# A two-layer hybrid mixer on one core: four PSUM banks for background projections, a reordered inverse, and paired low-rank products

## The chip, the core and the metric

The kernel runs on one core of one Trainium2 chip. The metric is the device time of one execution in microseconds (us); lower is better. PE is the matmul engine (PEld is its weight load), DVE the vector engine, ACT the scalar engine, POOL the GpSimd engine, SP the engine that issues most DMA transfers. PSUM, into which PE writes, has 8 banks of 128 partitions by 512 float32.

## What is computed

Two layers of a diffusion backbone over 768 tokens (256 context, then 512 latent) of width 1024. In each layer four mixers read one normalised input through one large projection `w_in`; each mixer's result is lifted to width 1024, weighted by a sigmoid gate that is also computed from the input, summed, and projected again; an MLP follows. The mixer that matters here is branch B, a bidirectional recurrence with four heads of 64:

```python
# per direction d, per head; kk is the normalised key, b = kk * a
w = -softplus(-(w0[d] + tanh(wl) @ w2[d])) - 0.5          # decay
a = sigmoid(a0[d] + al @ a2[d])                           # rate
S_t = S_{t-1} (diag(exp(-exp(w_t))) - kk_t^T b_t) + v_t^T k_t
y_t = S_t r_t
```

`wl` and `al` hold 64 columns for the forward and 64 for the backward direction, and so do the rows of `w2` and `a2`.

## The kernel before, in words

**Products in three parts.** Nearly all projections take a split of both operands into a high and a low float32r part and three matmuls per 128 rows (`mm3_steps`, all recorded at line 387). Weights come by DMA from SP in halves of 128x512 (tile `wr`), ACT casts the high part (`wh`, line 258) and POOL or DVE subtracts for the low part (`wl`, line 259). Four raw and four split halves are kept, which is two projections' worth.

**Background work.** Branch B has long serial stretches. To fill PE, `fill(t)` draws steps from generators: `spill` (projections of other mixers, rotated, split and stored to DRAM), `gates`, `ada_steps` (the modulation vectors, 16 loads and 8 row additions each, mixed into `spill`), and `decays`. A projection's result sits in a PSUM tile `pm` of the pool `psm` (2 banks) until ACT copies it out (`st`, line 504, or `gate`). The call `fill` stands at fixed places of branch B with fixed amounts (table `FILL`); whatever is left of `spill` is run at the end of the branch. The instructions of one engine run in the order in which the scheduler of the framework has put them, which mostly follows the program and lets an instruction pass earlier ones that it holds to be not ready.

**Branch B** (`branch_b`) uses 4 banks of its own pool `bbp` for everything and 2 of pool `bbc` for the state products `pst`. In order of time:

1. Nine projections of the input, each followed by the token shift (`shift`, lines 769 to 780): ACT copies `pm` twice (`xp`, `xm`), DVE adds and scales. Between them the steps of `prep(0)` for the first pair of heads: norm of the keys (`early`), the low-rank products of decay and rate with tanh out of PSUM (`decay`, tiles `plo`), and the element products on 128x768 (`elem`). The last two projections of the list `todo` are 5 (values of the second pair, `vv[1]`) and 1 (receptance of the second pair, `r1`). `r1` is stored to DRAM (`rd`, line 955), since its buffer, tag `gb`, becomes the tile `gb` of the next step.
2. For each pair `hp` of heads: the Gram products (`pgr`), masked by DVE into `gb` and `gk`; then the inverse of 64x64 unit triangles for 24 chunk-heads. It solves the 32x32 diagonal blocks in 31 steps of two DVE instructions (lines 1095, 1097, on the tile `xm`, called `yt` there), with `fill` and one step of `side()` (products that don't need the inverse, among them `pkt`, its copy `kt`, `pnz`, `pat`) behind each step.
3. When the 31 steps are through, DVE transposes the blocks into `xu` (line 1111), two copies on DVE and two on ACT put them into `gb` (line 1114), DVE transposes once more into `xz` (line 1117, same buffer as `xu`), and PE forms the off-diagonal block in two rounds, `pq` (line 1136) and `pz` (line 1150).
4. Products with the inverse (`ppu`, `pnu`, `per`), ten state hops (`pst`, line 1205, and a DVE addition each), the outputs `po`. During the first pair's steps the function `go` runs `prep(1)`, `early` and `decay` between the stages; `elem` follows after the hops.

In `ada_steps`, groups 3 and 4 (and their two transposes, line 304) stand directly behind the last row addition on DVE (line 290).

Of the kernel before, what the change touches and what calls it, by code (L numbers as in the profile page):

```python
# [9 lines left out]
F32 = mybir.dt.float32  # L10
F32R = mybir.dt.float32r
ALU = mybir.AluOpType
ACTF = mybir.ActivationFunctionType
AX = mybir.AxisListType
PSUM = bass.MemoryType.PSUM
# [7 lines left out]
DEPTH = 2  # L23
# [29 lines left out]
def prepare(inp):  # L53

    f = lambda n: np.asarray(inp[n])
    ar = {}
# [1 line left out]
    ar["ctx"] = f("ctx")[0]  # L58
    ar["cc"] = np.concatenate([f("c")[0].reshape(8, 128), f("c_ctx").reshape(8, 128)], 0)
    ar["ada"] = f("ada_w").reshape(DEPTH, 8, 128, 6, 1024).transpose(0, 3, 1, 2, 4)  # L60
    ar["w_in"] = f("w_in").reshape(DEPTH, 8, 128, 57, 128).transpose(0, 3, 2, 1, 4).reshape(DEPTH, 57, 128, 1024)
    ar["w_up"] = f("w_up").reshape(DEPTH, 8, 128, 32, 128).transpose(0, 3, 2, 1, 4).reshape(DEPTH, 32, 128, 1024)
    ar["w_down"] = f("w_down").reshape(DEPTH, 16, 2, 128, 2, 512).transpose(0, 1, 4, 3, 2, 5).reshape(DEPTH, 16, 2, 128, 1024)
    ar["w_out"] = f("w_out").reshape(DEPTH, 8, 128, 1024)
    ar["w_br"] = f("w_branch").reshape(DEPTH, 4, 2, 128, 2, 4, 128).transpose(0, 1, 4, 3, 5, 2, 6).reshape(DEPTH, 4, 2, 128, 1024)
    ar["w2"] = f("rwkv_w2").reshape(DEPTH, 128, 256)
    ar["a2"] = f("rwkv_a2").reshape(DEPTH, 128, 256)
    ar["g2"] = f("rwkv_g2")

    gp = np.stack([f("norm_post_mix"), f("norm_post_mlp")], 1)  # L70
# [8 lines left out]
    def put(name, a):  # L79
        o, w = PV[name]  # L80
        pv[:, :, o:o + w] = a
# [3 lines left out]
    put("gmix", cols(f("norm_pre_mix")))  # L85
    put("gmlp", cols(f("norm_pre_mlp")))
    put("adab", cols(f("ada_b")))
    put("mu", cols(f("rwkv_mu")))
    put("w0", cols(f("rwkv_w0")))
    put("a0", cols(f("rwkv_a0")))  # L90
    put("kk", cols(f("rwkv_kk")))
# [66 lines left out]
class Build:  # L158
    def __init__(self, tc, I, out):
        self.tc, self.nc, self.I, self.out = tc, tc.nc, I, out  # L160
        self.pool_split = 0
        self.filler, self.owed = [], 0.0

    def run(self):
        with ExitStack() as es:
# [5 lines left out]
    def pool(self, name, bufs=1, **kw):  # L171
        return self.es.enter_context(self.tc.tile_pool(name=name, bufs=bufs, **kw))
# [90 lines left out]
    @staticmethod  # L263
    def cols(u, a, n):

        h, o = a // 512, a % 512
        return u[h][0][:, o:o + n], u[h][1][:, o:o + n]


    def ada_steps(self, l, g, psum, tag, pool=None, parts=1):  # L270


        nc = self.nc
        kn = 8 // parts
        row = self.small.tile([128, 256], F32, tag="modrow", name="modrow", bufs=1)
        for k in range(8):
            if k % kn == 0:
                ps = psum.tile([128, 512], F32, tag=tag, name="pada")
            for h in range(2):
                raw = (pool or self.wraw).tile([128, 512], F32, tag="wr", name="wr")  # L280
                nc.sync.dma_start(raw, self.I["ada"][l, g, k][:, 512 * h:512 * h + 512])
                for i in range(2):
                    j = 2 * h + i
                    nc.tensor.matmul(ps[32 * j:32 * j + 32, 0:256], self.silu[:, k, :], raw[:, i * 256:(i + 1) * 256],  # L284
                                     start=k % kn == 0, stop=k % kn == kn - 1, tile_position=(0, 32 * j))
                if k % kn == kn - 1 and h == 1:
                    if k < kn:
                        nc.scalar.copy(row, ps[:, 0:256])
                    else:
                        nc.vector.tensor_tensor(row, row, ps[:, 0:256], ALU.add)  # L290
                if (k < 7 or h < 1) and (h or parts < 8):
                    yield 0.25 if parts < 8 else 0.5
        if g in (2, 5):

            s = g // 3
            gb = (pool or self.wraw).tile([128, 512], F32, tag="wr", name="gtb")
            nc.sync.dma_start(gb, self.I["gt"][l, s])
            nc.vector.tensor_tensor(row, row, gb[:, 0:256], ALU.add)
            nc.vector.tensor_tensor(row, row, gb[:, 256:512], ALU.mult)
            for j in range(4):  # L300
                nc.sync.dma_start(self.gtrow[l, s, :, j * 256:(j + 1) * 256], row[32 * j:32 * j + 2, :])
        else:
            for b in range(2):
                nc.tensor.transpose(ps[:, 256 + b * 128:256 + (b + 1) * 128], row[:, b * 128:(b + 1) * 128], self.idn)
            o, _ = PV["adab"]
            nc.vector.tensor_tensor(
                self.mod[:, l, 8 * g:8 * g + 8, :].rearrange("p (j b) w -> p j b w", j=4),
                ps[:, 256:512].rearrange("p (b j w) -> p j b w", b=2, j=4)[:, :, :, 0:2],
                self.pv[l][:, o + 8 * g:o + 8 * g + 8].rearrange("p (j b) -> p j b", j=4).unsqueeze(3).to_broadcast([128, 4, 2, 2]),
                ALU.add)  # L310
        yield 0.5
# [78 lines left out]
    def mm3(self, *a, **k):  # L390
        for _ in self.mm3_steps(*a, **k):
            pass

    def proj_steps(self, u, seg):

        o, n = seg
        ps = self.psm.tile([128, 512], F32, tag="m", name="pm")
        for k in range(8):
            yield from self.mm3_steps(ps[:, 0:n], self.cols(u, k * 128, 128), (self.hh[:, k, o:o + n], self.hl[:, k, o:o + n]),
                                      start=k == 0, stop=k == 7)  # L400
        return ps

    def proj(self, u, seg):
# [50 lines left out]
    def spill(self, l, cols):  # L454
# [6 lines left out]
        late, owed = [], []  # L461

        def rotated(st, tab, rot):
            pr = self.psm.tile([128, 512], F32, tag="m", name="prot")
            nc.tensor.matmul(pr, rot, st, start=True, stop=True)
            rt = self.stage.tile([128, 512], F32, tag="sl", name="rt")
            nc.vector.tensor_tensor(rt, pr, tab[:, 1, :], ALU.mult)
            nc.gpsimd.tensor_tensor(st, st, tab[:, 0, :], ALU.mult)
            nc.gpsimd.tensor_tensor(st, st, rt, ALU.add)
# [312 lines left out]
    def branch_b(self, l, start, more):  # L782
# [11 lines left out]
        with ExitStack() as es:  # L794
            pool = lambda n, b=1, **k: es.enter_context(tc.tile_pool(name=n, bufs=b, reuse_waits="tile", **k))
            keep = pool("bb", side="right")
            bps = pool("bbp", 4, space=PSUM)
            pch = pool("bbc", 1, space=PSUM)
            start(bps)
            ybuf = self.y  # L800
            pes = ExitStack()
# [43 lines left out]
            def decay(hp, d):  # L845

                vw = rev if d else nat
                dr, hs = half[d], slice(128 * hp, 128 * hp + 128)
                lw = bp.tile([128, T], F32, tag="t0", name="lw")
                cum = bp.tile([128, T], F32, tag="t1", name="cum")  # L850
                ta = bp.tile([128, T], F32, tag="t3", name="ta")
                for wt, src, dst, bias in ((w2, twl, lw, self.w0h), (a2, xal, ta, self.a0h)):
                    for o, n in SEGS:
                        ps = bps.tile([128, 512], F32, tag="m", name="plo")
                        nc.tensor.matmul(ps[:, 0:n], wt[dr, hs], src[dr, o:o + n], start=True, stop=True)
                        nc.scalar.activation(vw(dst[:, o:o + n]), nat(ps[:, 0:n]), ACTF.Tanh, scale=0.5,
                                             bias=bias[:, l, 2 * d + hp:2 * d + hp + 1])
                        yield
                c = -0.5 * math.exp(-0.5)
                nc.vector.tensor_scalar(lw, lw, 1.0, c, ALU.add, ALU.mult)  # L860
                yield
                nc.vector.tensor_tensor_scan(cum, smask, lw, 0.0, ALU.mult, ALU.add)
                yield
                nc.vector.tensor_tensor(lw, cum, lw, ALU.subtract)
                return lw, cum, ta
# [75 lines left out]
            sgl = keep.tile([128, T], F32, tag="z", name="sgp")  # L941
            r1 = keep.tile([128, T], F32, tag="gb", name="br_")
            kvr[1] = [ybuf[:, 1, :], vv[1], r1]
            todo = [(0, qsegs, r), (4, SEGS, vv[0]), (8, qsegs, sgl), (3, SEGS, ybuf[:, 1, :]), (5, SEGS, vv[1]), (1, qsegs, r1)]
            for n, (ti, segs, out) in enumerate(todo):
                u = self.unit(self.I["w_in"][l, TB + ti])
                for seg in segs:
# [3 lines left out]
                if ti == 8:  # L951
                    nc.scalar.activation(sgl[:, sl], sgl[:, sl], ACTF.Tanh, scale=0.5)
                    nc.vector.tensor_scalar(sgl[:, sl], sgl[:, sl], 1.0, 0.5, ALU.add, ALU.mult)
                    nc.sync.dma_start(self.sgd[:, sl], sgl[:, sl])
            nc.sync.dma_start(self.rd[:, sl], r1[:, sl])
            while next(state["gen"], self) is not self:
                self.fill(self.fl["pre"])

            for hp in range(2):
# [147 lines left out]
                    sgl = late.tile([128, T], F32, name="sgl")  # L1107
                    nc.sync.dma_start(sgl[:, sl], self.sgd[:, sl])

                xu = keep.tile([128, 32, 32], F32, tag="xu", name="xu")  # L1110
                nc.vector.transpose(out=xu.rearrange("p u t -> p t u"), in_=yt)
                for q in range(4):
                    qr = slice(32 * q, 32 * q + 32)
                    (nc.scalar.copy if q % 2 else nc.vector.tensor_copy)(
                        gb[qr, :, :, 0, 32 * (q % 2):32 * (q % 2) + 32], xu[qr, 0:24, :].rearrange("p (a b) t -> p a b t", b=2))
                xz = keep.tile([128, 32, 32], F32, tag="xu", name="xz")
                nc.vector.transpose(out=xz.rearrange("p u t -> p t u"), in_=yt.rearrange("p a b -> p b a"))

# [11 lines left out]
                for u0 in (0, 12):  # L1130
                    for d in range(2):
# [6 lines left out]
                        if d:  # L1138
                            nc.scalar.activation(dst, src, ACTF.Copy, scale=-1.0)
                        else:  # L1140
                            nc.vector.tensor_scalar(dst, src, -1.0, None, ALU.mult)
                go(2)
                self.fill(self.fl["z"])
                for u0 in (0, 12):
# [53 lines left out]
                    go(2)  # L1198
                self.fill(self.fl["er"])

                pst = [pch.tile([128, 512], F32, tag=f"c{i}", name="pst") for i in range(2)]
                for s in range(1, 11):
                    for d in range(2):
                        for i, ri in enumerate(half):
# [33 lines left out]
            for hp in range(2):  # L1238
                for o, n, prs in self.stat_rows(keep, bps, rs[:, hp], qsegs, "z", 1, "btail"):
# [4 lines left out]
                    nc.tensor.matmul(ps[:, 0:n], g2[:, 128 * hp:128 * hp + 128], sgl[:, o:o + n], start=True, stop=True)  # L1244
                    nc.vector.tensor_tensor(y, y, ps[:, 0:n], ALU.mult)
            self.run_all(self.sp)


    def branch_a(self, l):
# [539 lines left out]
```

## Time and profile before

| what | value |
|---|---|
| median of 3 runs | 2825.8 us (2818.15 to 2826.36) |
| the profiled execution | 2828.87 us, span 2826.7 us |
| mean granted PE clock | 0.964 |
| branch B, layer 0 | from about 62 to 461 us of the span |
| branch B, layer 1 | from about 1633 to 2022 us |

Times in the profile count from the span's start. A row of the timeline names the instruction's line, what it writes and reads, and in brackets the engine's idle time before it with the instruction that ended the idle time. A row of the waits names who waited for whom: us in total, times, and the longest.

### The profile page before, as it was taken

Reading aid. Unit: us, or ns where it says so; the run is one execution under the profiler, and the core shown is the slowest. Engines: PE = TensorE matmul, PEld = TensorE weight load, DVE = VectorE, ACT = ScalarE, POOL = GpSimd, SP = SyncE. Lnnn points to the kernel's source line nnn. Section 1 sums busy time; section 2 is a strip of 40 time slices with the busy share of each in tenths; the row PEclk is TensorE's granted clock in tenths of the full one; section 3 lists DMA queues with packets and bytes.
Section 4 is the critical chain, followed back from the end, with each engine's and each line's share of the span. In section 5 each row is a group of like instructions: output and inputs, shape, how many; then the busy total and the mean of one; then the engine's idle time right before and its main releaser. Section 6 shows DMA issues by size and latency. Waiting matters only on the chain.

```text
span 2826.7 us, 44263 instructions
## 1 busy us (share of the span) xinstructions
PE 2645.2 (94%) x17093; PEld 2112.2 (75%) x17093; DVE 1474.8 (52%) x2520; ACT 1080.7 (38%) x2136; POOL 765.3 (27%) x825
## 2 busy tenths in 40 slices
PE   6889899999999999999999878888999999999998
PEld 3776577888788778888888766657688686778886
DVE  4675662475836542333334558676166865434444
ACT  3432262464446333222223343235255464333232
POOL 3423436222421321011111543332622422101012
PEclk8988999999999999999999989898999999999999
DMA  6123545434533532322222212254545536342222
GB/s 218 45 91 98 182 147 175 126 114 142 179 109 109 164 112 90 101 90 90 90 90 88 91 65 69 94 179 153 181 136 171 173 109 192 121 144 95 93 93 94
DMA packets 177778, 346.52 MB, mean 123 GB/s; under 512 B 19440, under 2 KB 33312, under 8 KB 177568
## 3 DMA queue, kind: packets, MB, share of 16 engines
q1 hardware_dynamic: 139680, 279.99, 30.6%
q10 hardware_dynamic: 30208, 44.97, 4.5%
q0 software_dynamic: 7680, 18.75, 2.5%
q8 instruction: 134, 2.20, 0.3%
q14 instruction: 76, 0.62, 0.1%
HBM read 280.55 MB, written 63.08 MB: 122 GB/s over the span
## 4 chain that ended last, share of the span: by engine, by line
PE 73%; DVE 12%; POOL 4%; DMA 4%; ACT 3%; issue 3%; SPq 0%; ACTq 0%; POOLq 0%; DVEq 0%
PE pm L387 39%; PE pd L387 15%; PE pwo L387 4%; PE plift L387 2%; DVE xm L1097 2%; DVE tmp L1095 1%; PE pada L284 1%; PE ppu L1161 1%; PE pay L561 1%; PE pas L1297 1%; POOL merged L1487 1%; PE pcy L561 1%; PE pdy L561 1%; DMA wr<-ada 1%; PE paw L1319 1%
## 5 line engine op out<-in xcount | busy, mean ns | idle before, releaser
L387 PE MATMUL pm<-hh,wh 128*128 128x512 f32 (+1 forms) x2272 | 830.2, 366 | 24.5 <-ACT st L504 10.6
L387 PE MATMUL pm<-hl,wh 128*128 128x512 f32 (+1 forms) x2272 | 819.5, 361 | 6.3 <-POOL hl L1575 5.0
L387 PE MATMUL pm<-hh,wl 128*128 128x512 f32 (+1 forms) x2272 | 819.8, 361 | 5.1 <-POOL wl L259 4.3
L258 ACT CAST wh<-wr 128x512 fp32r<-128x512 f32 x516 | 318.4, 619 | 704.6 <-PE pm L387 289.1
L387 PEld LDWEIGHTS pm<-hh,wh 128*128 128x128 f32 x2272 | 437.9, 193 | 120.4 <-issue 25.2
L259 DVE TENSOR_TENSOR wl<-wr,wh 128x512 fp32r<-128x512 f32 x348 | 248.3, 716 | 497.9 <-ACT wh L258 495.1
L387 PEld LDWEIGHTS pm<-hl,wh 128*128 128x128 f32 x2272 | 438.8, 193 | 75.5 <-issue 9.2
L387 PEld LDWEIGHTS pm<-hh,wl 128*128 128x128 f32 x2272 | 438.8, 193 | 71.4 <-POOL wl L259 5.7
L259 POOL TENSOR_TENSOR wl<-wr,wh 128x512 fp32r<-128x512 f32 x168 | 231.0, 1379 | 410.1 <-ACT wh L258 373.1
L1700 POOL TENSOR_TENSOR s<-r 128x256 f32<-128x256 f32 (+1 forms) x98 | 91.5, 934 | 757.7 <-ACT r L1699 754.5
L387 PE MATMUL pd<-wh,sh 128*128 128x512 f32 x640 | 253.4, 397 | 1.1 <-DVE hf L374 0.5
L387 PE MATMUL pd<-wl,sh 128*128 128x512 f32 x640 | 253.3, 396 | 0.0
L387 PE MATMUL pd<-wh,sl 128*128 128x512 f32 x640 | 253.0, 396 | 0.1
L1702 DVE TENSOR_TENSOR sl<-s,sh 128x256 fp32r<-128x256 f32 (+1 forms) x98 | 58.0, 592 | 177.5 <-POOL s L1700 177.5
L387 PEld LDWEIGHTS pd<-wh,sh 128*128 128x128 f32 x640 | 120.4, 188 | 34.9 <-ACT wh L258 3.3
L387 PEld LDWEIGHTS pd<-wh,sl 128*128 128x128 f32 x640 | 120.6, 188 | 28.9 <-DVE sl L1702 0.5
L387 PEld LDWEIGHTS pd<-wl,sh 128*128 128x128 f32 x640 | 120.6, 188 | 28.3 <-DVE wl L259 0.2
L1746 DVE TENSOR_TENSOR acc<-acc,pd 128x512 f32<-128x512 f32 x120 | 82.3, 686 | 51.7 <-PE pd L387 50.6
L1487 POOL TENSOR_TENSOR merged<-merged,gateb 128x256 f32<-128x256 f32 (+1 forms) x72 | 88.2, 1230 | 76.5 <-DVE gateb L1486 71.7
L1699 ACT ACTIVATE r<-pm 128x256 f32<-128x256 f32 (+1 forms) x98 | 50.5, 516 | 118.5 <-PE pm L387 118.4
L387 PE MATMUL plift<-yh,wh 128*128 128x256 f32 (+1 forms) x192 | 72.9, 379 | 7.3 <-DVE gateb L1486 3.6
L1301 ACT ACTIVATE ae<-pas,asum 128x768 f32<-128x768 f32 (+1 forms) x80 | 65.2, 818 | 34.1 <-DVE asum L1299 31.5
(386 smaller groups left out, 4051.6 us busy)
## 6 DMA issues: line engine op xcount, KB each, us to landing
wr<-w_in SPq DMA_DIRECT2D x228, 256.0 KB, 2.9
wr<-ada SPq DMA_DIRECT2D x192, 256.0 KB, 3.0
wr<-w_up SPq DMA_DIRECT2D x128, 256.0 KB, 2.9
wr<-w_down SPq DMA_DIRECT2D x128, 256.0 KB, 2.8
graw<-gate ACTq DMA_DIRECT2D x64, 256.0 KB, 3.7
x<-x SPq DMA_DIRECT2D x28, 512.0 KB, 5.9
gateb<-graw SPq DMA_DIRECT2D x32, 384.0 KB, 3.5
wr<-w_br SPq DMA_DIRECT2D x32, 256.0 KB, 2.8
```

What stands on the lines that cost most here:

```text
L258: nc.scalar.copy(hi, raw)
L259: (nc.gpsimd if self.pool_split > h else nc.vector).tensor_tensor(lo, raw, f32(hi), ALU.subtract)
L284: nc.tensor.matmul(ps[32 * j:32 * j + 32, 0:256], self.silu[:, k, :], raw[:, i * 256:(i + 1) * 256], start=k % kn == 0, stop=k % kn == kn ...
L387: self.nc.tensor.matmul(ps, a[u], b[v], start=start and i == 0, stop=stop and i == 2)
L561: self.nc.tensor.matmul(py, v.rearrange("p e d -> p (e d)"), w[i], start=start and i == 0, stop=stop and i == 1)
L1097: nc.vector.tensor_tensor(yt[:, j + 1:, 0:j + 1], yt[:, j + 1:, 0:j + 1], tm, ALU.subtract)
L1301: nc.scalar.activation(e[:, 0:nkc], ps[:, 0:nkc], ACTF.Exp, bias=sums[:, c:c + 1], accum_out=sums[:, 2 + c:3 + c])
L1487: nc.gpsimd.tensor_tensor(mo, mo, t, ALU.add)
L1699: nc.scalar.activation(r[:, 0:n], ps[:, 0:n], ACTF.Relu)
L1700: nc.gpsimd.tensor_tensor(s2[:, 0:n], r[:, 0:n], r[:, 0:n], ALU.mult)
L1702: nc.vector.tensor_tensor(s[1][:, o:o + n], s2[:, 0:n], f32(s[0][:, o:o + n]), ALU.subtract)
L1746: nc.vector.tensor_tensor(a, a, po[t - t0], ALU.add)
```

## The change

Four edits. (a) The pool `bbc` goes; two banks `bbx` come in its place, and background tiles (`pm`, `prot`) alternate between `psm` and `bbx` as long as branch B lasts; `pst` takes two of the four banks of `bbp`. (b) The pair of transposes is exchanged: `xz` comes first, then `pq`, and `xu` with its four copies stands behind `pq`; `xu` moves to the buffer of `z`, which the products `pnz` read last. (c) The rows of `a2` and of the matching projection are exchanged on the host, so that decay and rate of one direction lie in different row halves; `decay` issues the two products of one segment back to back into two banks, then the two tanh. (d) Projection 1 comes before projection 5, and the store of `r1` directly behind it. Also, `ada_steps` yields once between the last row addition and the transposes, and at the end the branch draws background steps until no projection is under way.

```diff
+    def bank(self, name):
+        self.turn ^= 1
+        return (self.extra if self.extra and self.turn else self.psm).tile([128, 512], F32, tag="m", name=name)
...
-        ps = self.psm.tile([128, 512], F32, tag="m", name="pm")
+        ps = self.bank("pm")
+        self.held += 1
...
-            pr = self.psm.tile([128, 512], F32, tag="m", name="prot")
+            pr = self.bank("prot")
...
-            pch = pool("bbc", 1, space=PSUM)
+            self.extra = pool("bbx", 2, space=PSUM)
...
+            if parts == 8:
+                yield 0.1
             for b in range(2):
                 nc.tensor.transpose(ps[:, 256 + b * 128:256 + (b + 1) * 128], row[:, b * 128:(b + 1) * 128], self.idn)
...
-                for wt, src, dst, bias in ((w2, twl, lw, self.w0h), (a2, xal, ta, self.a0h)):
-                    for o, n in SEGS:
-                        ps = bps.tile([128, 512], F32, tag="m", name="plo")
-                        nc.tensor.matmul(ps[:, 0:n], wt[dr, hs], src[dr, o:o + n], start=True, stop=True)
-                        nc.scalar.activation(vw(dst[:, o:o + n]), nat(ps[:, 0:n]), ACTF.Tanh, scale=0.5,
+                both = ((w2, twl, lw, self.w0h, half[d]), (a2, xal, ta, self.a0h, half[1 - d]))
+                for o, n in SEGS:
+                    ps = [bps.tile([128, 512], F32, tag="m", name="plo") for _ in both]
+                    for p, (wt, src, dst, bias, dr) in zip(ps, both):
+                        nc.tensor.matmul(p[:, 0:n], wt[dr, hs], src[dr, o:o + n], start=True, stop=True)
+                    for p, (wt, src, dst, bias, dr) in zip(ps, both):
+                        nc.scalar.activation(vw(dst[:, o:o + n]), nat(p[:, 0:n]), ACTF.Tanh, scale=0.5,
                                              bias=bias[:, l, 2 * d + hp:2 * d + hp + 1])
                         yield
...
-            todo = [(0, qsegs, r), (4, SEGS, vv[0]), (8, qsegs, sgl), (3, SEGS, ybuf[:, 1, :]), (5, SEGS, vv[1]), (1, qsegs, r1)]
+            todo = [(0, qsegs, r), (4, SEGS, vv[0]), (8, qsegs, sgl), (3, SEGS, ybuf[:, 1, :]), (1, qsegs, r1), (5, SEGS, vv[1])]
...
-            nc.sync.dma_start(self.rd[:, sl], r1[:, sl])
+                if ti == 1:
+                    nc.sync.dma_start(self.rd[:, sl], r1[:, sl])
...
-                xu = keep.tile([128, 32, 32], F32, tag="xu", name="xu")
-                nc.vector.transpose(out=xu.rearrange("p u t -> p t u"), in_=yt)
-                for q in range(4): ...
                 xz = keep.tile([128, 32, 32], F32, tag="xu", name="xz")
                 nc.vector.transpose(out=xz.rearrange("p u t -> p t u"), in_=yt.rearrange("p a b -> p b a"))
...
+                xu = keep.tile([128, 32, 32], F32, tag="z", name="xu")
+                nc.vector.transpose(out=xu.rearrange("p u t -> p t u"), in_=yt)
+                for q in range(4): ...
                 go(2)
                 self.fill(self.fl["z"])
...
-                pst = [pch.tile([128, 512], F32, tag=f"c{i}", name="pst") for i in range(2)]
+                pst = [bps.tile([128, 512], F32, tag="m", name="pst") for i in range(2)]
...
+            self.extra = None
+            while self.held:
+                self.fill(0.1)
```

## Rows read from the trace of the kernel before

**Rows 1.** The page: busy time, share of the span and instructions of each engine.

```profile
PE 2645.2 (94%) x17093; PEld 2112.2 (75%) x17093; DVE 1474.8 (52%) x2520; ACT 1080.7 (38%) x2136; POOL 765.3 (27%) x825
```

**Rows 2.** Windows, branch B: length; PE, PEld, DVE, ACT, POOL busy; granted clock; DMA.

```profile
62.00:461.00 399.00, 358.35 (x3668) 275.67 (x3668) 245.68 (x435) 146.54 (x282) 161.34 (x166) 0.92 0.35 115
1633.00:2022.00 389.00, 333.47 (x3346) 248.55 (x3346) 254.44 (x427) 143.78 (x273) 151.17 (x146) 0.89 0.34 113
```

**Rows 3.** Waits of PE in layer 0's branch B (62 to 461 us).

```profile
PE pnz L1070 <- ACT kt L1060: 7.3, 2, 4.0
PE pm L387 <- ACT xm L777: 4.4, 2, 4.1
PE pm L387 <- POOL wl L259: 4.3, 3, 2.2
PE pada L304 <- DVE modrow L290: 4.2, 2, 2.6
...
PE pgr L973 <- DVE gb L980: 3.1, 3, 2.8
```

**Rows 4.** Waits of PE in layer 1's branch B (1660 to 2022 us).

```profile
PE pm L387 <- ACT st L504: 10.6, 3, 6.8
PE pq L1136 <- DVE xz L1117: 7.4, 1, 7.4
PE pada L304 <- DVE modrow L290: 6.0, 2, 5.0
...
PE pm L387 <- ACT xm L777: 2.8, 2, 2.6
```

**Rows 5.** Timeline of ACT around the first stall of the shifts, layer 0.

```profile
138.40 0.37 ACT L775 COPY xp<-pm 128x256 f32<-128x256 f32 x1 [7.22 <-DVE xt L779]
...
141.01 1.13 ACT L258 CAST wh<-wr 128x512 fp32r<-128x512 f32 x2
```

**Rows 6.** Timeline of DVE at the first masked Gram products of both layers.

```profile
165.86 1.29 DVE L980 TENSOR_TENSOR gb<-pgr,c_gmask 128x512 f32<-128x512 f32 x2 [3.80 <-DMA rd<-br__838]
...
1734.45 1.89 DVE L980 TENSOR_TENSOR gb<-pgr,c_gmask 128x512 f32<-128x512 f32 x3 [2.36 <-DMA rd<-br__15759]
```

**Rows 7.** Timeline of ACT at the end of an inverse: layer 0, then layer 1, first pair.

```profile
211.91 1.67 ACT L1114 COPY gb<-xu 32x768 f32<-32x768 f32 x2 [3.88 <-DVE xu L1111]
213.60 0.59 ACT L1060 COPY kt<-pkt 128x512 f32<-128x512 f32 x1
...
1782.64 0.83 ACT L1114 COPY gb<-xu 32x768 f32<-32x768 f32 x1 [7.12 <-DVE xu L1111]
```

**Rows 8.** Timeline of DVE and PE at the ends of layer 1's two inverses.

```profile
1780.65 1.90 DVE L1111 STREAM_TRANSPOSE xu<-xm 128x1024 f32<-128x1024 f32 x1
...
1788.74 1.49 PE L1136 MATMUL pq<-xz,gb 32*32 32x32 f32 x27
...
1924.71 1.90 DVE L1111 STREAM_TRANSPOSE xu<-xm 128x1024 f32<-128x1024 f32 x1
...
1928.98 2.05 DVE L1117 STREAM_TRANSPOSE xz<-xm 128x1024 f32<-128x1024 f32 x1 [1.21 <-ACT gb L1114]
```

**Rows 9.** Windows behind three PE stalls, columns as in rows 2.

```profile
213.50:220.40 6.90, 6.16 (x51) 4.63 (x52) 2.70 (x3) 3.04 (x7) 3.88 (x5) 0.52 0.49 169
1780.20:1797.30 17.10, 13.16 (x138) 10.58 (x139) 9.45 (x15) 3.84 (x6) 3.07 (x5) 0.51 0.28 92
1927.00:1947.50 20.50, 16.42 (x225) 14.51 (x227) 7.93 (x12) 10.22 (x19) 2.54 (x2) 0.51 0.19 65
```

**Rows 10.** Windows of tile pq alone (PE, PEld, DVE, ACT), layer 0, then layer 1.

```profile
220.00:250.00 30.00, 2.92 (x96) 2.81 (x96) 1.10 (x2) 0.96 (x2) 0.82 0.29 85
...
1928.00:1955.00 27.00, 4.76 (x96) 4.63 (x96) 1.10 (x2) 0.96 (x2) 0.64 0.33 107
```

**Rows 11.** Windows of tile plo alone, sum over the eight decay stages.

```profile
sum 154.00, PE 27.91 PEld 10.99 ACT 17.36; mean PE 3.49 PEld 1.37 ACT 2.17
```

**Rows 12.** Timeline of PE: two Gram blocks in a row on four quadrants.

```profile
159.73 1.98 PE L973 MATMUL pgr<-big,bk 64*64 64x128 f32 x64
```

More of the change, by code (lines that the diff above doesn't have):

```diff
@@ L60, in prepare @@
     ar["ada"] = f("ada_w").reshape(DEPTH, 8, 128, 6, 1024).transpose(0, 3, 1, 2, 4)
-    ar["w_in"] = f("w_in").reshape(DEPTH, 8, 128, 57, 128).transpose(0, 3, 2, 1, 4).reshape(DEPTH, 57, 128, 1024)
+    ar["w_in"] = f("w_in").reshape(DEPTH, 8, 128, 57, 128).transpose(0, 3, 2, 1, 4).reshape(DEPTH, 57, 128, 1024).copy()
     ar["w_up"] = f("w_up").reshape(DEPTH, 8, 128, 32, 128).transpose(0, 3, 2, 1, 4).reshape(DEPTH, 32, 128, 1024)
@@ L66, in prepare @@
     ar["w2"] = f("rwkv_w2").reshape(DEPTH, 128, 256)
-    ar["a2"] = f("rwkv_a2").reshape(DEPTH, 128, 256)
+    swap = np.r_[64:128, 0:64]
+    ar["a2"] = f("rwkv_a2").reshape(DEPTH, 128, 256)[:, swap]
+    ar["w_in"][:, TB + 7] = ar["w_in"][:, TB + 7].reshape(DEPTH, 128, 8, 128)[..., swap].reshape(DEPTH, 128, 1024)
     ar["g2"] = f("rwkv_g2")
@@ L87, in prepare @@
     put("adab", cols(f("ada_b")))
-    put("mu", cols(f("rwkv_mu")))
+    mu = cols(f("rwkv_mu")).copy()
+    mu[:, :, 7] = mu[:, swap, 7]
+    put("mu", mu)
     put("w0", cols(f("rwkv_w0")))
@@ L162, in __init__ @@
         self.filler, self.owed = [], 0.0
+        self.extra, self.turn, self.held = None, 0, 0
     def run(self):
@@ L400, in proj_steps @@
                                       start=k == 0, stop=k == 7)
+        self.held -= 1
         return ps
@@ L847, in decay @@
                 vw = rev if d else nat
-                dr, hs = half[d], slice(128 * hp, 128 * hp + 128)
+                hs = slice(128 * hp, 128 * hp + 128)
                 lw = bp.tile([128, T], F32, tag="t0", name="lw")
@@ L1108, in branch_b @@
                     nc.sync.dma_start(sgl[:, sl], self.sgd[:, sl])
-                xu = keep.tile([128, 32, 32], F32, tag="xu", name="xu")
-                nc.vector.transpose(out=xu.rearrange("p u t -> p t u"), in_=yt)
[L1112 to L1115, printed above, removed]
                 xz = keep.tile([128, 32, 32], F32, tag="xu", name="xz")
@@ L1141, in branch_b @@
                             nc.vector.tensor_scalar(dst, src, -1.0, None, ALU.mult)
+                xu = keep.tile([128, 32, 32], F32, tag="z", name="xu")
+                nc.vector.transpose(out=xu.rearrange("p u t -> p t u"), in_=yt)
+                for q in range(4):
+                    qr = slice(32 * q, 32 * q + 32)
+                    (nc.scalar.copy if q % 2 else nc.vector.tensor_copy)(
+                        gb[qr, :, :, 0, 32 * (q % 2):32 * (q % 2) + 32], xu[qr, 0:24, :].rearrange("p (a b) t -> p a b t", b=2))
                 go(2)
```

## The prediction

> **What bounds the kernel now.** I read the page first, then the waits of PE, the timelines of PE, ACT and DVE around each longer wait, and the windows for the granted clock. The page shows PE busy for 94% of the span [rows 1]: over the whole kernel PE is the bound, and the background steps that fill branch B have to be run anyway, so a microsecond in which PE stands idle is worth about a microsecond, and one in which it is busy is not to be had except by fewer or shorter matmuls. All four edits lie in branch B. In its two stretches PE is busy 358.35 of 399 us and 333.47 of 389 [rows 2]: 40.7 and 55.5 us idle, 96 in all. The granted clock there is 0.92 and 0.89, so part of the busy time is at the lower of PE's two levels (1.2 instead of 2.4 GHz). This is the stock from which the change can draw. The waits name its pieces [rows 3, 4]; I take those that an edit touches and ask each time what is late next.
>
> **The edits, part by part.**
>
> Shifts (four banks). PE waits 4.4 us in layer 0 and 2.8 in layer 1 for ACT to empty `pm` into `xm` [rows 3, 4], 7.2 in all. With four banks PE needn't wait for that copy. But ACT itself stands 7.22 us for DVE's `xt`, and the casts of the next weights come behind it, at 141.01 [rows 5]: PE soon wants those weights. So most of the wait turns into one for `wh`. Between 0 and 7.2 I take 3.0.
>
> Gram (order of 1 and 5). DVE's first mask waits 3.80 and 2.36 us for the store of `r1` [rows 6], because `gb` takes its buffer; PE's wait behind it is up to 2.8 us [rows 3]. With projection 5 between, the store has a whole projection and its shift to land in, 24 matmuls for each segment. SP is passed by one more store at this place; the weights of projection 5 are queued before it if the scheduler keeps its habit, as the loads are ready earlier. DVE's chain starts earlier by 6.2 in all; between 2.8 and 6.2 I take 5.5.
>
> End of the inverse, layer 0. ACT runs in order, and the copy `gb<-xu` stands ahead of the third `kt` copy: it waits 3.88 us for DVE's transpose, and `kt` follows at 213.60 [rows 7]. PE's `pnz` wait for it, 7.3 us in the two inverses [rows 3]. After the change `xu` lies in the buffer that `pnz` read, so it can't be ahead of `kt` any more. After the first wait PE has 6.9 us at a granted 0.52 [rows 9], so about half of it, 3.4 us, is loss too. The weight casts and `st` copies behind on ACT come free as well. Between 3.6 (half of the waits stay) and 10.7 I take 9.5.
>
> End of the inverse, layer 1. Here DVE is later than PE. First pair: `xu` starts at 1780.65; in its place comes `xz`, 2.05 us, so `pq` can start at 1782.70 instead of 1788.74, 6.0 us earlier [rows 8]. The 6.8 us for which PE waits for `st` [rows 4] lie before it, on ACT behind the same kind of copy, which waits 7.12 [rows 7]; with four banks PE is through with its work before 1782.7, and the rest of this wait is taken up by `pq`, so it isn't counted again. Second pair: `xz` moves from 1928.98 to 1924.71, 4.3 us. A shorter stall remains before `pq` in both. Behind both stalls the clock is 0.51 for 17.10 and 20.50 us [rows 9]; the 96 matmuls of `pq` take 4.76 us there and 2.92 in layer 0 [rows 10]. If the clock holds, that gives 1.8 for each of `pq` and, of like size, the second pair's `pz`. Between 10.3 and 16 I take 11.5.
>
> The clock is told in the Trainium skill too, in "TensorE: Matmul & The Clock Gate", section "Terms": the price of a throttled stretch is its length times one minus the ratio. By that rule the stretches of rows 9 would give back 22 us, where I count 5 to 6 of them. The trace agrees on the half rate (4.76 against 2.92, with small matmuls that hide part of it); that all of it comes back it does not show.
>
> Tail of layer 1's branch. The other two waits of `pm` for `st`, 10.6-6.8 = 3.8 us [rows 4], are plain bank waits. I take 3.5 of 0 to 3.8.
>
> The yield in `ada_steps`. PE waits 4.2 and 6.0 us for the last row addition [rows 3, 4]; in its place now come nine or eleven background matmuls. Of layer 0's, 2.6 lie inside an inverse and should go. The rest lies where `elem` loads DVE and POOL, and where PE also waits for `wl`, 4.3 us [rows 3]; there PE only comes earlier to the next wait. Between 0 and 10.2 I take 3.5. The row's bank is kept a little longer, of which nothing else has need.
>
> Paired low-rank products. Eight stages keep PE busy 27.91 us [rows 11]. The trace has no pair of 64x128 products on different row halves; the nearest is the Gram block, 64 matmuls on four quadrants in 1.98 us, 31 ns each for 128 columns [rows 12], less than 128 columns at 2.4 GHz would take one after the other (53 ns), so quadrants do overlap. At best half, 14.0 us, at worst nothing. These products stand between background matmuls that keep PE in order, and ACT needs 17.36 us for their tanh. I take 3.0.
>
> On this the Trainium skill has a rule that speaks against the edit: "TensorEngine Tiling (Array Packing)", section "PSUM Bottleneck", says tiling makes the matmuls faster but not the emptying of PSUM. By that rule the stages would be worth 27.91-17.36 = 10.6 us at most, not 14.0; no run shows the pair yet.
>
> Sum of gains: 3.0+5.5+9.5+11.5+3.5+3.5+3.0 = 39.5 us.
>
> Costs. `pst` now waits for a bank that `pnu` or `per` must give back, one DVE eviction of a few tenths at four places, hidden if it is a bank of `pnu`: the row nearest is 1.29/2 = 0.65 for a 128x512 mask [rows 6]; 0 to 2.6, I take 1.0. Behind it on PE stand only hops and background. `pz` now needs `xu`: if DVE transposes it while PE does `pq`, 1.90 us against 2.92, nothing; if it comes behind `pq`, 1.90 plus two ACT copies of 0.83 [rows 7, 8], 3.6 us at four places, 14 in all. Cover is one `fill` of 1.0 and, for the first pair, key norms. DVE is free at that moment and the scheduler has let ready instructions pass (the early `gb<-xu` shows it), so I take 3.0. The draining loop at the end costs nothing: its matmuls are due anyway.
>
> Net 39.5-4.0 = 35.5. The profiled execution took 2828.87 us, 3.1 above the median of 2825.8; from it 2793.4, from the median **2790**.
>
> **Rivals.**
>
> *Weights bound the background.* Banks and yield only bring PE earlier to the next wait for a cast or a `wl`. For: rows 5, and 4.3 us of waits for `wl` already. Against: in the inverses PE waits for no weights in these rows. The first, fifth, sixth and seventh terms fall away: 26.5-4.0 = 22.5, which gives 2803.
>
> *Partners bound it.* In these stretches ACT, POOL and DVE end each stage, and PE waits elsewhere for the same end. Only what shortens their own chain stays: the store (5.5) and the exchange on DVE in the second inverse (4.3), less costs of 4.0: 5.8, so 2820, within what can be told from no change. For: DVE is the late one at both `pq` of layer 1. Against: PE's 94%, and in layer 0 `pnz` waits for a copy that had nothing to do.
>
> *The ACT queue is held longer, slower.* The place is the copy `gb<-xu` on ACT. If it keeps its early place there, it now waits for `xz`, `pq` and its eviction as well, 2.05+2.92+0.55 = 5.5 us more than today's 3.88 to 7.12, at four places; `st` and casts behind it stop, PE runs out of weights and goes to the low clock, some 3.4 us each. The third and fourth term (21.0) fall away and 4x8.9 = 36 come on top: -39.5+21.0+36+4 = +21, so 2847. It breaks even at 14.5/4 = 3.6 us per place and is slower beyond. Against: the buffer of `z` keeps the copy behind `pnz`.
>
> **How the numbers follow.** My forecast has 0.62, weights 0.18, partners 0.12, the held queue 0.08. About 0.3% (8.5 us) is what this kernel's measurement can tell from none: faster 0.80, same 0.12, slower 0.08. With all upper bounds the gain is 7.2+6.2+10.7+16+3.8+10.2+14.0 = 68, with few of the low ones about 5; I leave out the outer ends and the slower case: 2760 to 2820.
>
> **What would show it.** Right: no PE wait for `xm`, `rd` or `st` above 1 us in branch B; `pnz` without a wait for `kt`; `xz` ahead of `xu` on DVE, and `xu` during `pq`; `pq` of layer 1 about 2.1 us behind the last `yt` step; branch B's idle time down from 96 to about 65 us, with a clock above 0.92 in layer 1. Wrong: new waits of PE for `wl` or `wh` of 2 us and more at the old places, ACT idle before `gb<-xu` as long as now, `pz` waiting for `gb`, or stages outside branch B that have changed by more than 2 us.

## The result

The changed kernel takes 2791.9 us (median of 4 runs, 2790.6 to 2794.6) against 2824.0 us of the kernel before on the same chip: ratio 0.989 [0.9878, 0.9903], some 31 us less. The forecast was 2790. The profiled execution took 2794.6 us with a span of 2792.8. In what follows a ratio is turned into microseconds by its distance from 1 times 2824.

The total did come out as forecast, but not all of its terms did; the profile after shows this first. The page, as in [rows 1]:

```profile
PE 2622.6 (94%) x17093; PEld 2096.2 (75%) x17093; DVE 1473.4 (53%) x2520; ACT 1082.2 (39%) x2136; POOL 770.7 (28%) x825
```

The number of instructions is the same; PE is busy 22.6 us less. The windows of branch B in both layers, to be read beside [rows 2]. They begin and end at the same products of the branch; of the background between them they hold a few matmuls less or more:

```profile
63.00:438.00 375.00, 343.30 (x3663) 265.96 (x3662) 251.69 (x435) 147.00 (x282) 163.84 (x166) 0.94 0.37 122
1612.00:1986.00 374.00, 325.36 (x3362) 245.97 (x3363) 247.61 (x427) 143.56 (x274) 155.16 (x146) 0.90 0.36 118
```

The two stretches are 24 and 15 us shorter, 39 in all, and some 5 us are lost outside them, since the span is 34 us shorter: the whole gain lies in branch B. But PE's idle time there only fell from 96 to 31.7+48.6 = 80 us; the other 23 are busy time, for nearly the same number of instructions. The granted clock rose from 0.92 to 0.94 and from 0.89 to 0.90. The waits of PE in layer 0, then layer 1, beside [rows 3, 4]:

```profile
PE pm L395 <- POOL wl L265: 6.7, 5, 4.1
...
PE pnz L1088 <- ACT kt L1078: 2.3, 2, 1.6
PE pgr L991 <- DVE gb L998: 1.7, 5, 1.0
...
PE pz L1169 <- DVE gb L1170: 1.4, 1, 1.4
...
PE pada L312 <- DVE modrow L296: 1.2, 1, 1.2
...
PE pada L312 <- DVE modrow L296: 8.2, 2, 4.7
...
PE pm L395 <- POOL wl L265: 6.3, 3, 3.4
PE prot L480 <- ACT st L519: 6.0, 1, 6.0
```

Gone are the waits for `xm` (4.4 and 2.8), those of `pm` for `st` (10.6) and of `pq` for `xz` (7.4). `pnz` waits 2.3 instead of 7.3 us. A `prot` in layer 1 waits 6.0 us for `st`, where it waited 1.8, and there are more waits for `wl`: 6.7 instead of 4.3 in layer 0, and 6.3 in layer 1, where there was none. The waits for the row addition of `ada_steps` are 9.4 us in the two layers together, 10.2 before. DVE's masks no longer wait for the store of `r1`: the timeline has six in a row without idle time ahead of them, where [rows 6] had 3.80 and 2.36 us:

```profile
155.65 3.79 DVE L998 TENSOR_TENSOR gb<-pgr,c_gmask 128x512 f32<-128x512 f32 x6
...
1707.62 3.79 DVE L998 TENSOR_TENSOR gb<-pgr,c_gmask 128x512 f32<-128x512 f32 x6
```

The timelines of DVE, and then of PE, at the end of layer 1's first inverse, beside [rows 8]:

```profile
1748.68 2.23 DVE L1129 STREAM_TRANSPOSE xz<-xm 128x1024 f32<-128x1024 f32 x1
1750.82 1.98 DVE L1156 STREAM_TRANSPOSE xu<-xm 128x1024 f32<-128x1024 f32 x1
```

```profile
1755.54 0.28 PE L395 MATMUL pm<-hl,wh 128*128 128x256 f32 x1
1755.75 2.92 PE L1148 MATMUL pq<-xz,gb 32*32 32x32 f32 x96
```

`xz` is done at 1750.9, but PE comes to `pq` only at 1755.75, out of background work with hardly a gap. So the roles have changed: DVE was late before, PE is late now, by 4.8 us. That is why `xu` lies ahead of `pq` and not under it, and why nothing more is to be had at this place from a faster DVE.

### The profile page after: what moved, and what is told of

Same layout as the page of the kernel before. It is cut to its first block, busy times and chain, and to the rows that moved or that the text cites. A ratio compares the mean times of both kernels' runs of the same rounds, so it can differ in the third digit from the quotient of the medians.

```text
span 2792.8 us, 44256 instructions
## 1 busy us (share of the span) xinstructions
PE 2622.6 (94%) x17093; PEld 2096.2 (75%) x17093; DVE 1473.4 (53%) x2520; ACT 1082.2 (39%) x2136; POOL 770.7 (28%) x825
## 4 chain that ended last, share of the span: by engine, by line
PE 71%; DVE 10%; POOL 3%; DMA 3%; ACT 3%; issue 2%; ACTq 0%; SPq 0%; DVEq 0%; POOLq 0%
PE pm L395 38%; PE pd L395 15%; PE pwo L395 4%; PE plift L395 2%; PE pada L290 1%; DVE tmp L1113 1%; DMA gateb<-graw 1%; DVE xm L1115 1%; PE ppu L1180 1%; POOL merged L1510 1%; PE pay L576 1%; PE pas L1320 1%; PE pdy L576 1%; PE pcy L576 1%; PE paw L1342 1%
```

## The experiments

**Each edit alone, on the kernel before.** Which of the four pays, and do they add up?

Banks (with `pst` in the pool of four and the drain at the end of branch B):

```
-        ps = self.psm.tile([128, 512], F32, tag="m", name="pm")
+        ps = self.bank("pm")
...
-            pch = pool("bbc", 1, space=PSUM)
+            self.extra = pool("bbx", 2, space=PSUM)
```

> The kernel before with edit (a) alone: two more banks for background tiles, pst in the recurrence's pool. Theory of the prediction (terms by stage): shift stalls 3.0 plus tail of layer 1 3.5 less 1.0 for pst, 5 to 6 us faster, and some of the 6.8 us wait for st in layer 1's first inverse, so 5 to 10 us; PE's waits for xm and st gone from branch B. Rival, weights bound the background: 0 to 2 us, with PE's waits for wl or wh grown by about what xm and st lost. Rival, pst costs: slower by 1 to 3 us, seen in PE's wait of pst for DVE.

Exchange (`xu` behind the eviction of `pq`, in the buffer of `z`):

```
-                xu = keep.tile([128, 32, 32], F32, tag="xu", name="xu")
...
+                xu = keep.tile([128, 32, 32], F32, tag="z", name="xu")
```

> The kernel before with edit (b) alone: xz and pq ahead of xu, xu in the buffer of z. Theory of the prediction: 9.5 plus 11.5 less 3.0, 18 us faster (12 to 24); no wait of pnz for kt above 1 us in layer 0, pq of layer 1 about 2.1 us behind the last step of the inverse. Rival, partners bound the stages: 4 to 6 us, the waits come back at pz (for gb) or later. Rival, the held ACT queue: slower by 10 us or more, ACT idle before gb<-xu for over 8 us.

Order of the projections, with the store of `r1` behind its own:

```
-            todo = [..., (5, SEGS, vv[1]), (1, qsegs, r1)]
+            todo = [..., (1, qsegs, r1), (5, SEGS, vv[1])]
```

> The kernel before with edit (d) alone: projection 1 before projection 5, its store directly behind it. Theory of the prediction: 5.5 us faster (2.8 to 6.2), with no DMA wait in front of the first gb. Rival: the inverse hides it since PE is late there by more, 0 to 1 us although the first Gram mask starts 6 us earlier in the two layers together.

Paired decay and rate products:

```
+                both = ((w2, twl, lw, self.w0h, half[d]), (a2, xal, ta, self.a0h, half[1 - d]))
```

> The kernel before with edit (c) alone: decay and rate products of one direction on both row halves, back to back in two banks. Theory of the prediction: 3.0 us faster (0 to 14); PE busy in plo falls from 27.9 to about 20 us if pairs overlap. Rival, row halves don't overlap for these products: busy in plo stays at 27 to 28 us and the time within 1 us of the kernel before.

| alone | ratio to before | us |
|---|---|---|
| banks | 0.9972 [0.9958, 0.9985] | -7.9 |
| exchange | 0.9992 [0.9978, 1.0007] | -2.3 |
| order of projections | 0.9978 [0.9965, 0.999] | -6.2 |
| paired products | 0.9977 [0.9964, 0.9989] | -6.5 |

Together 22.9 us, where the changed kernel has 31. The exchange, from which I had expected most (18 us), brings nothing that can be told from none.

The banks' 7.9 us lie within the 5 to 10 that I expected, but not where I put them. Windows from the first `prs` (a product in the norm of the keys) to the first `pgr`, layer 0 and then layer 1, which hold the shifts with all of the 7.2 us of waits for `xm` (columns as in [rows 2]): the kernel before, the banks alone, the changed kernel without the banks (a run of the next part), the changed kernel:

```profile
98.93:159.73 60.80, 56.41 (x273) 45.42 (x273) 38.40 (x43) 23.71 (x44) 26.63 (x34) 0.93 0.15 50
1678.30:1729.80 51.50, 48.62 (x218) 38.18 (x218) 37.82 (x39) 20.73 (x37) 23.52 (x29) 0.90 0.16 52
...
97.70:152.60 54.90, 54.87 (x273) 44.30 (x273) 39.16 (x43) 23.65 (x44) 26.61 (x34) 0.94 0.17 56
1666.70:1711.80 45.10, 45.10 (x214) 35.85 (x214) 35.87 (x38) 20.73 (x37) 22.36 (x27) 0.96 0.14 48
...
97.90:157.20 59.30, 53.82 (x273) 43.55 (x273) 41.70 (x43) 23.74 (x44) 27.11 (x34) 0.92 0.19 65
1657.10:1710.90 53.80, 47.29 (x216) 37.39 (x216) 38.69 (x39) 20.59 (x37) 24.58 (x29) 0.88 0.18 59
...
97.24:153.40 56.16, 54.23 (x273) 43.93 (x273) 42.06 (x43) 23.62 (x44) 27.49 (x34) 0.91 0.20 63
1658.70:1704.70 46.00, 43.10 (x218) 34.67 (x218) 37.68 (x37) 20.13 (x36) 24.52 (x27) 0.96 0.16 53
```

The sums are 112.3, 100.0, 113.1 and 102.2 us. The banks make the shifts 11 to 12 us shorter, as much as they bring in all, or more; PE's idle time there is gone with the banks alone (7.3 us to none), and the rest is busy time, in layer 1 at a granted clock of 0.96 instead of 0.90.

Why the exchange brings so little, the traces show for one place, the end of layer 1's first inverse. Waits of PE there with the exchange alone, and ACT's rows ahead of the first:

```profile
1778.43 0.58 PE L387 MATMUL pm<-hh,wh 128*128 128x256 f32 x1 [6.50 <-ACT st L504]
1783.02 4.76 PE L1130 MATMUL pq<-xz,gb 32*32 32x32 f32 x96
...
1776.92 0.83 ACT L1141 COPY gb<-xu 32x768 f32<-32x768 f32 x1 [7.86 <-DVE xu L1138]
1777.78 0.60 ACT L504 ACTIVATE st<-pm 128x512 f32<-128x512 f32 x1
```

With the banks alone:

```profile
1769.98 4.74 PE L1144 MATMUL pq<-xz,gb 32*32 32x32 f32 x96 [6.96 <-DVE xz L1125]
```

Two waits stand side by side here, one for a bank and one for DVE, and PE stands once for the later of them. Take away either, and PE stands 6.5 to 7 us for the other; in both kernels `pq` takes 4.7 us, as in [rows 10]. The wait for a bank is one for DVE too, at one remove: `st` stands on ACT behind `gb<-xu`, which waits 7.86 us for the transpose `xu`. In layer 0 the exchange alone does take `pnz`'s wait for `kt` from 7.3 to 1.7 us, with a new wait of 2.7 us of `pat` for ACT's `sn`; why no more of that comes out in the time stays open.

**Exchange and banks together, and the changed kernel without one of them.** If that is so, both together bring more than their sum, and in the changed kernel each is worth more than alone.

> The changed kernel, but with the exchange xu back at its old place (ahead of xz, in its own buffer order). Alone the later exchange brought about 2 us. If the parts simply add, this kernel lies about 2 us behind the changed one, 0.990 of the kernel before. If the exchange pays only together with the extra banks (without them PE stands at the same moment for a bank whose st copy ACT has not made), the loss is 10 to 14 us, 0.993 to 0.994, with a wait of pnz for kt of 3 to 4 us in layer 0 and of pq for xz of about 7 us twice in layer 1 in the profile.

> The changed kernel with the background on its two old PSUM banks and pst in its own two. Alone the banks brought about 8 us. If the parts add, this kernel is at 0.992. If banks and exchange need each other, it loses 14 to 18 us, 0.994 to 0.9955, and the wait of PE for st of 6 to 7 us in layer 1's first inverse is back, with pq behind it and no wait of its own.

> The kernel before with the banks and the later exchange together, and neither the new order of the projections, nor the yield, nor the paired products. Alone they brought 8 and 2 us. If they need each other (each takes away the wait that would take the other's place), both together bring 16 to 19 us, 0.9935 to 0.9945, and what the changed kernel has beyond the sum of its parts is explained. If they only add, 10 us, 0.9965.

The edits are those above, put back or applied as a pair.

| kernel | ratio to before | us |
|---|---|---|
| changed, without the exchange | 0.9925 [0.9906, 0.9944] | -21.2 |
| changed, without the banks | 0.9928 [0.9906, 0.995] | -20.3 |
| before, with banks and exchange | 0.9938 [0.9921, 0.9955] | -17.5 |

The pair brings 17.5 us against 7.9+2.3 = 10.2 alone. Left out of the changed kernel, the exchange costs some 10 us instead of 2, the banks 11 instead of 8. Every one of these intervals is 5 to 6 us wide to each side, and each surplus is a difference of several of them, so by the times alone the pair's surplus, some 7 us, is no larger than its own uncertainty. The three comparisons have one sign, and the pair's waits for `pq` are small in the trace:

```profile
1765.53 1.57 PE L1138 MATMUL pq<-xz,gb 32*32 32x32 f32 x48 [0.80 <-DVE xz L1119]
1767.48 1.42 PE L1138 MATMUL pq<-xz,gb 32*32 32x32 f32 x24 [0.38 <-DVE modrow L291]
1770.58 1.48 PE L1138 MATMUL pq<-xz,gb 32*32 32x32 f32 x24 [1.69 <-DVE modrow L291]
```

What shows the surplus is the stretch itself, from the first `pgr` to the first `pq` of layer 1 (starts in PE's timeline):

| kernel | first `pgr` | first `pq` | us between |
|---|---|---|---|
| before | 1729.77 | 1788.74 | 59.0 |
| banks alone | 1711.82 | 1769.98 | 58.2 |
| exchange alone | 1722.90 | 1783.02 | 60.1 |
| banks and exchange | 1712.51 | 1765.53 | 53.0 |
| order of projections alone | 1717.48 | 1769.28 | 51.8 |
| changed, without the exchange | 1709.48 | 1761.85 | 52.4 |
| changed, without the banks | 1710.89 | 1764.48 | 53.6 |
| changed | 1704.66 | 1755.75 | 51.1 |

Alone neither edit shortens it; together they take 6 us off. Two kernels with another edit that doesn't touch this place (`pst` and the paired products, each alone) are at 58.8 and 59.1, so 6 us are clear of the spread. But in the changed kernel each of the two is worth only 1 to 2.5 us here, because the new order of the projections alone already takes 7 off. Their larger worth there lies elsewhere: the banks' in the shifts (113.1 against 102.2 us above), the exchange's in good part in layer 0, where `pnz` waits 6.2 us for `kt` without it and 2.3 with it.

With 17.5 for the pair, 6.2 and 6.5 for the other two, 30.2 of the 31 us are accounted for, within intervals that together come to some 7 us. Not all of my expectation held: without the banks the loss is 11 us, nearer to the 8 of parts that add than to 14 to 18; without the exchange `pq` waits 1.4 and 2.9 us for `xz`, not 7 each, and without the banks the wait for `st` is 2.8, not 6 to 7.

**The yield in `ada_steps`.** The changed kernel without it:

```
-            if parts == 8:
-                yield 0.1
```

> The changed kernel without the yield in ada_steps. The profile of the changed kernel still shows waits of the modulation's transposes (1.24, 3.49 and 4.69 us) and new ones for wl (4.11, 3.42), so I expect no difference: 0.989, within 2 us of the changed kernel. The rival is that the yield is what the four other edits alone do not account for, about 8 us: then this kernel is at 0.992.

0.9898 [0.9881, 0.9915], 2 us from the changed kernel and within the interval. Its waits of PE, in layer 0 and then layer 1:

```profile
PE pm L393 <- POOL wl L265: 4.7, 5, 2.0
...
PE pada L310 <- DVE modrow L296: 2.8, 1, 2.8
...
PE pm L393 <- POOL wl L265: 5.3, 3, 2.5
PE pada L310 <- DVE modrow L296: 4.5, 2, 3.4
```

Without the yield PE waits 7.3 us for the row addition and 10.0 for `wl`; with it 9.4 and 13.0. The yield has not shortened that wait. DVE adds the row late, behind the inverse's or `elem`'s work, and a few more background matmuls do not reach that far. So it is at the longest of these waits in the changed kernel:

```profile
1889.16 1.21 DVE L1115 TENSOR_TENSOR xm<-xm,tmp 128x60 f32<-128x60 f32 x1
1890.29 0.41 DVE L296 TENSOR_TENSOR modrow<-modrow,pada 128x256 f32<-128x256 f32 x1
```

**The banks of `pst`.** The kernel before with the place of `pst` changed and the pool `bbc`, then without use, left out:

```
-                pst = [pch.tile([128, 512], F32, tag=f"c{i}", name="pst") for i in range(2)]
+                pst = [bps.tile([128, 512], F32, tag="m", name="pst") for i in range(2)]
```

> The kernel before with one thing changed: the recurrence's two pst banks come from the pool of four that the other blocks share. This is the cost that I set at 1.0 us (0 to 2.6): ratio 1.000 to 1.001, with PE waiting at the first pst for an eviction of at most a few tenths. The rival: the pool of four becomes short and other blocks wait for it, 3 us and more, 1.001 and above.

1.0002 [0.9991, 1.0013]: it costs nothing that can be measured. PE stands for 0.3 and 0.2 us ahead of `pnu`, behind DVE's `big`, and at no `pst` for a bank.

**What of the paired products pays: the rows' halves or the order?** Both products of a pair on the same half, once in the changed kernel and once alone in the kernel before:

```
-                both = (..., (a2, xal, ta, self.a0h, half[1 - d]))
+                both = (..., (a2, xal, ta, self.a0h, half[d]))
```

> The changed kernel with decay and rate products in the new order, two banks at once, but both on the same half of the rows as before (no exchange of the halves of a2, its projection and mu). If the gain of about 6 us comes from the two products running on PE at the same time, this kernel is 4 to 7 us slower than the changed one, 0.991 to 0.9915, and the second product of a pair starts when the first ends. If it comes from the order alone (PE gets a bank earlier, ACT finds two banks full), it is the same, 0.989.

> The kernel before with the decay and rate products in the new order (both for a segment, into two banks, then both tanh), but both on the same half of the rows. With the halves it brought about 6.5 us. If the order makes the gain, 0.997 to 0.998 again; if the row halves make it (PE busy 16.65 instead of 27.91 us on these products), 0.999 to 1.0005, with PE busy about 27 us on them.

The windows of `plo` alone over both branches (PE, PEld, ACT), to be read beside [rows 11]. The changed kernel:

```profile
sum 773.00, PE 16.95 PEld 6.53 ACT 17.05; mean PE 8.47 PEld 3.27 ACT 8.53
```

The changed kernel on one half:

```profile
sum 773.00, PE 26.76 PEld 11.69 ACT 17.63; mean PE 13.38 PEld 5.85 ACT 8.81
```

The order alone, in the kernel before:

```profile
sum 773.00, PE 26.76 PEld 11.97 ACT 17.67; mean PE 13.38 PEld 5.99 ACT 8.84
```

On different halves the two products do run at the same time: PE is busy 16.95 instead of 27.91 us. Of these 11 us little comes out in the time. The changed kernel on one half is at 0.9893 [0.9875, 0.9911], no different from the changed kernel. The order alone is at 0.9992 [0.998, 1.0004], where order and halves gave 0.9977 [0.9964, 0.9989]. So the halves are worth some 1 us by the first pair of kernels and 4 by the second, and the intervals allow none in both. How much it is stays open; that it is not 11 is shown. ACT needs 17 us for its tanh in any of them. The Trainium skill, "TensorEngine Tiling (Array Packing)", section "PSUM Bottleneck", says that tiling speeds up the matmuls and not the emptying of PSUM. The rows agree: ACT 17.36 before and 17.05 after. That ACT is what hides the saving is not shown by these runs.

**The tail.** The changed kernel with `st` copied out of its bank ahead of what is left of the block before:

```
-                if late:
-                    late.pop()()
                 st = self.gst.tile([128, 512], F32, tag="st", name="st")[:, 0:n]
                 nc.scalar.activation(st, ps[:, 0:n], ACTF.Copy, scale=scale)
+                if late:
+                    late.pop()()
```

> The changed kernel with one line moved: in the projections that are stored for the attention branches, ACT copies a block out of its bank (st) before the copy and the stores of the block before it, not behind them. In the tail of layer 1 PE waits 5.99 us for this st, which on ACT stands behind a copy and two stores that wait for POOL. If that is the place where the gain of the tail went, the wait goes and the kernel is 3 to 6 us faster than the changed one, 0.987 to 0.988. If POOL bounds the tail anyway, PE only waits at the next block, and it is the same within 2 us, 0.989.

0.9889 [0.9868, 0.9909], and the same wait. The timeline of ACT at this place in this kernel:

```profile
1959.54 0.62 ACT L489 CAST sth<-st 128x512 fp32r<-128x512 f32 x1 [4.16 <-POOL st L484]
1960.19 0.33 ACTq L497 DMA_DIRECT2D stk<-sth  x1
1961.56 0.33 ACTq L497 DMA_DIRECT2D stk<-stl  x1
1961.93 0.38 ACT L517 ACTIVATE st<-pm 128x256 f32<-128x256 f32 x1 [1.77 <-POOL stl L490]
1962.21 0.61 ACT L264 CAST wh<-wr 128x512 fp32r<-128x512 f32 x1
1965.83 0.62 ACT L489 CAST sth<-st 128x512 fp32r<-128x512 f32 x1 [3.01 <-POOL st L484]
```

ACT takes its instructions in the same order as in the changed kernel, and its idle times differ by 0.01 us: moving the line has not moved the copy, which still stands behind the store of `stl` that waits for POOL. So this run doesn't test the idea; whether the tail can be shortened stays open. What the rows do show is the chain: ACT's `sth` waits 4.16 and 3.01 us for POOL's `st`, and the next `st`, which PE wants, stands behind it.

## Why the prediction was right, and where its steps were not

**The stock.** Right that the gain lies in branch B and that a wait on the chain of PE is worth its length. Wrong in kind: I looked for 31 us less idle time and a clock above 0.92 in layer 1. Idle time fell by 16, busy time by 23, of which 11 are `plo`; the clock is 0.90 in layer 1. The other 12 fit the clock: by the granted clocks of both layers' windows I estimate that PE spent some 150 us at the lower level before (twice 0.08 of 399 us and twice 0.11 of 389) and 120 after, which at half the speed is some 15 us of work. I had counted 5 to 6 us for the clock, at other places.

**Shifts, 3.0.** The largest error of size. The waits for `xm`, 7.2 us, are gone, and in the changed kernel PE then waits for the next weights, as I said: `wl` 1.75 us in layer 0 and 1.36 and 1.49 in layer 1. By these waits 2.6 us would stay. But the stretches with the shifts are 10 to 12 us shorter with the banks, beyond my upper end of 7.2: with the banks alone no wait for weights came in place of the old ones, and I had not counted the busy time that goes with the clock.

**Gram, 5.5.** Right: the order alone brings 6.2 us, and DVE's wait is gone.

**Ends of the inverses, 9.5 and 11.5.** The waits that I named did go, but the sizes were far too large. With the terms of the shifts and the tail and the costs, banks and exchange were to bring 3.0+9.5+11.5+3.5-4.0 = 23.5; the pair measures 17.5 [12.7, 22.3], and 12 of it lie in the shifts by the pair's trace (54.7 and 45.1 us from `prs` to `pgr`). In the changed kernel the exchange is worth 10 us where I had 18. In layer 0 `pnz` still waits 2.3 us where I had none. In layer 1 PE is through 4.8 us later than `xz`: there PE's own work is the next limit, and I counted as if it were DVE. So `pq` starts 7.1 and 4.8 us behind the last step of layer 1's two inverses, not 2.1. What I had right is that the wait for `st` and the one for `pq` mustn't be counted twice; what I did not say is the reverse, that at this place neither edit has a gain without the other.

**The clock in it.** I gave 1.8 us for each `pq`, and for the second pair's `pz`, "if the clock holds". `pq` is at 2.92 us in all four places. `pz` is not: it takes 4.77 in three of them; see below.

**Tail, 3.5.** The step that failed outright. I called the waits for `st` plain bank waits. With four banks PE does not stand for a bank; it stands at the next `prot` for the `st` of the next block, since ACT itself is held by POOL. PE's rows of this `prot`, before and after:

```profile
2014.78 1.13 PE L465 MATMUL prot<-st,rot 128*128 128x512 f32 x2 [1.81 <-ACT st L504]
...
1976.82 2.07 PE L480 MATMUL prot<-st,rot 128*128 128x512 f32 x2 [5.99 <-ACT st L519]
```

By the waits nothing is gained: 3.8 us at `pm` and 1.8 at `prot` have become 6.0 at `prot`.

**Yield, 3.5.** Mis-sized: not to be told from nothing, and the wait it was to fill is 9.4 instead of 10.2 us.

**Paired products, 3.0.** The paired kernel alone brings 6.5 us; the halves, which I costed, 1 to 4 of it. That they overlap and that most of it is hidden was right.

**Costs, 4.0.** `pst` costs nothing measurable, 1.0 in the sum. `pz` waits for `gb` once, 1.4 us, where I took 3.0. In the sum the inverses, the tail and the yield were sized too high, the shifts and the paired products too low; 35.5 us were forecast from the profiled execution, and 31 measured. That the errors cancel so nearly is in part luck.

**The rivals.** The held ACT queue did not come in the changed kernel: ahead of the copy `gb<-xu` ACT is idle 1.92 and 5.56 us in layer 1 and not at all in layer 0, where it was 1.2 to 7.1 before (two of the four are in [rows 7]). Its place was well chosen all the same: with the exchange alone the copy keeps its place ahead of `st` at layer 1's first inverse, and ACT waits 7.86 us, longer than the 7.12 before. It waits for `xu` only, not for `pq` too, as DVE does `xu` directly behind `xz`. "Weights bound the background" is right for one of its four terms, the yield: waits for `wl` stand where those waits were, the longest 4.1 us. At the shifts such waits stand too, in the changed kernel, but the stretch is 10 us shorter all the same. It is wrong for the sum.

## What to carry to other kernels

Where two waits of one engine stand at the same place, for two different partners, each edit alone can measure as nothing, and only the pair shows what it is worth; test such edits together and by leaving one out, and see in the trace in which stretch the time went: a gain of the right size can lie in another place than the one it was forecast for. A wait that is called a bank wait goes away with more banks only if the engine that empties the bank is not itself held: look at what that engine waits for, and whether the next instruction needs the same copy. Busy time that is saved need not be time: of PE's 11 us on the paired products 1 to 4 came out.

## What was not expected of the hardware

In layer 1 the low clock behind the stalls of [rows 9] did not go with the stalls. It came behind `pq` instead. The windows from `pq` on in the changed kernel, layer 1, first pair, then second (columns as in rows 2):

```profile
1752.00:1755.70 3.70, 3.30 (x23) 1.99 (x21) 3.62 (x4) 2.26 (x3) 2.84 (x3) 1.00 0.53 188
1755.70:1758.70 3.00, 3.00 (x99) 2.91 (x97) 2.12 (x5) 0.00 (x0) 3.00 (x3) 1.00 0.00 0
1758.70:1761.00 2.30, 1.67 (x8) 1.37 (x8) 1.02 (x2) 0.49 (x1) 1.70 (x2) 0.56 0.80 228
...
1768.00:1772.00 4.00, 4.00 (x34) 2.90 (x34) 0.96 (x3) 0.85 (x2) 0.00 (x0) 0.50 0.02 4
1772.00:1776.00 4.00, 4.00 (x65) 3.74 (x63) 3.26 (x10) 1.95 (x6) 0.00 (x0) 0.92 0.55 178
...
1895.80:1898.80 3.00, 3.00 (x98) 2.93 (x98) 2.74 (x6) 2.03 (x5) 0.00 (x0) 1.00 0.42 160
1898.80:1902.00 3.20, 3.20 (x25) 2.26 (x26) 0.00 (x0) 2.17 (x4) 1.28 (x1) 0.52 0.21 80
1902.00:1906.00 4.00, 4.00 (x81) 3.94 (x80) 1.49 (x3) 1.39 (x3) 0.00 (x0) 0.50 0.57 180
```

During `pq` PE is busy the whole time at a granted 1.00; right behind it, it is at its lower level (1.2 GHz), in the second pair without an idle moment. `pz` then takes 4.77 us in both pairs, as `pq` did at this level in [rows 10]. The lower level lasts from about 1758.7 to 1772, some 13 us, and in the second pair some 10 us, where the profile before has 17.10 and 20.50 us behind the stalls: the stretches have moved and become shorter. What PE did ahead of them were 96 products of 32x32. No run here separates these small products from what else changed, so that they are the cause is not shown. The kernel before speaks both ways: in layer 0 its first `pq` ran at 0.99 and the 3.6 us behind it at 0.53, with PE busy throughout, but behind its second `pq` the clock stayed at 1.00. The Trainium skill, "TensorE: Matmul & The Clock Gate", section "Terms", prices such a stretch as its length times one minus the ratio. By that rule, as an estimate, 22 us were to be had if the low stretches of [rows 9] went. They went only in part and with other changes, so no run here tests the price.
